# One hybrid decoder layer on one core: a reordered first stage, the sine product on another engine, a border with slices beside every maximum, and earlier fetches of the output weights

## The chip, the cores and the metric

The kernel runs on one core of a Trainium2 chip. The metric is the device time of one execution in microseconds. The kernel before was timed three times: 1210.0, 1212.68 and 1214.48 us, median **1212.68 us**. The profiled execution took 1212.92 us, of which 1211.0 us are the span from the first to the last instruction; 1.9 us lie around it.

Engines: PE is the matrix engine (PEld its weight loads), DVE is VectorE, ACT is ScalarE, POOL is GpSimd, SP is SyncE, which issues most of the DMAs.

## The reference, cut to what matters

A layer over 2048 tokens of width 1024 with two attention branches. Branch A (FoX) is causal attention of 8 heads with a forget-gate bias; branch B (SWA) is attention in a window of 128 tokens, with rotary positions and sinks. Each branch has a SiLU gate, and one output projection joins them.

```python
mod = silu(c) @ w_ada + b_ada                      # shift, scale, gate
h = rms_norm(x, g_pre) * (1 + scale) + shift
qa, ka, va, fa, za, qb, kb, vb, zb = split(h @ w_in)
oa = forgetting_attention(qa, ka, va, fa + b_fgate) * silu(za)
qb, kb = rope(qb, positions), rope(kb, positions)
ob = sliding_window_sink_attention(qb, kb, vb, sinks) * silu(zb)
y = concat(oa, ob) @ w_out
x = x + gate * rms_norm(y, g_post)
```

## The kernel before, in words

**Number form.** Every large product is done in three half-precision matmuls: an operand is split into a high and a low f16 part. A projection weight therefore passes through events: `w_load` (DMA on POOL's queue), `w_max` (largest magnitude, L213), `w_back`, `w_scale` (a power of two, L232 to L239), `w_high` (ACT, L247), `w_low` (DVE, L253), `w_done`.

**First stage** (written out by hand in program order, 0 to 59.2 us). Sixteen halves of `w_ada` (tiles `wa`, 512 KB each, L437) come in on SP's queue, with the positions `posi` (L443) and the rotary frequencies `ifr` (L444) issued behind the first of them, tokens x0 to x3 in the middle, then the first piece of the gate weight `wr_zb` (L207; POOL's queue fetches the same piece once before, at 4.36 us), then x4 to x7, which lie in memory named `hT` until they are used. PE and DVE sum the products of `w_ada` (L473, L482, closing sums L590 and L591). `squares(0)` (ACT, L374) and `root(0)` (13 small DVE instructions, L93 to L107) give the norm of x0 to x3, `normal(0)` scales the tokens (L384), and the small sums L592 to L629 end in the column scale `Gp` (L626) and shift `Shp` (L627). Then eight turns, one for each 128 of the 1024 columns: PE transposes (`px`, L392), ACT scales into `hT` and `hf` (L398), DVE makes the split (L402, L403); with them runs the projection `kb` of the first 512 tokens (L309).

**Projections** (59.2 to 127.1 us; token chunks ci = 0, 1, 2 of 512 tokens, the fourth up to 159 us). The work is a list of slices `punits`; a chunk is 8 slices `kb` (rotary keys), 8 slices `vb` (values and forget logits, L750), 8 slices of the gate `zb` (L309), and between them 8 `turn_x` slices that prepare the next chunk. `events` hangs other work on slice numbers: the weight events, and `squares`, `root` and `normal` of the next chunk. Evacuations are pushed ahead in `after(n, ...)`, and a tick releases the next of them; here there is a tick at every second slice. After the projection, `kb` and later `qb` go through `evac_rope`: ACT copies (`qf`, L707), SP swaps the halves by DMA (`qs`, L709), DVE multiplies by the cosine (L712), POOL multiplies by the sine (L721), DVE adds (L722), ACT makes the high part (L723), DVE the low (L716). Each engine takes its instructions in program order.

**SWA** (158.9 to 445.4 us): 32 windows with the other gate, query and value slices between them, with the same `evac_rope`. The prefix sums of the forget logits (`sums`, L791 and L792) come just ahead of it, at 149 us.

**Border** (445.4 to 494.6 us). Key rows (`lk`, L1203, transposed in L1183), one small sum of `w_out` (L1123), the first slices of the FoX head 0 (`qk0`, 32 slices of three matmuls with 512 columns each, their results swapped into T by DMAs from `stq`), the last value slices, and 34 maxima. A maximum is one matmul (L1226) and one DVE reduction (L1229 or L1231); they start 14 slices before the end of `qk0`, and FoX's first step waits for all of them.

**FoX** (to 1004 us): 160 steps, each with scores (L1275 to L1278), the exponential on ACT (L1282, L1286), the low part on DVE (L1289) and the products with values (L1299 to L1302), and filler slices spread over them. From 951 us, in head 6 and 7, pieces of `w_out` come in (`wo`, L1359 on SP) and are split (L1368 on ACT, then DVE), one a step; a piece is fetched two steps ahead of its split, at the end of a step. **Output** (to 1211 us): the last product (L1428) and norm.

Of the kernel before, what the change touches and what calls it, by code (L numbers as in the profile page):

```python
# [41 lines left out]
def hybrid_layer(  # L42
# [47 lines left out]
    def rsqrt_mean(dst, ss, n):  # L90

        v = sm(n, "rs_v")
# [6 lines left out]
        for it in range(3):  # L99
            t = sm(n, "rs_t")  # L100
# [6 lines left out]
            V.scalar_tensor_tensor(y2[:], t[:], 1.5, y[:], op0=ALU.add, op1=ALU.mult)  # L107
            y = y2
# [271 lines left out]
    def normal(ci, us=range(4)):  # L380
        for u in us:
            t, r = ci * 4 + u, rstd[ci][1][:, u:u + 1]
            if ci == 0 or (ci == 1 and u % 2):
# [39 lines left out]
    with tc.manual_schedule():  # L423
# [15 lines left out]
        for k in range(1):  # L439
            load_ada(1, k)  # L440

        for g in range(4):
            SP.dma_start(posi[32 * g:32 * g + 32, :], positions[0, g * CH:(g + 1) * CH].partition_broadcast(32))  # L443
        SP.dma_start(ifr[:], inv_freq)  # L444
        for k in range(1, KT):
            load_ada(1, k)
        make_identity(nc, ident)
        for key in first:
# [112 lines left out]
        w_load("zb0", pieces("zb0"), SP)  # L561
        for t in range(4, 8):
            load_x(t)
        ada_sum(1, True)

        mx3 = st.tile([P, 2], F32, name="mx3")
        for n, key in enumerate(first[:2]):
            V.tensor_reduce(mx3[:, n:n + 1], wq[key][0][:], axis=AX.XY, op=ALU.max, apply_absolute_value=True)
        ada_pe(0, 0, True)
        ada_pe(0, 3)  # L570
        PE.transpose(bk[0][0:2, 0:P], mx3[:], ident[:])
        ada_pe(0, 5)
        ada_dve(0, 1, True)
        ada_dve(0, 2, False)
        squares(0)
        scl0 = col8("scl0")
        ada_col(1, scl0)
        root(0)
        normal(0)
# [5 lines left out]
        ada_dve(0, 4, False)  # L585
        ada_dve(0, 6, False)

        for n in range(2):
            nn = slice(n * CH, (n + 1) * CH)
            PE.matmul(pm[0][n][:], ones[:], acc[0][:, nn], start=False, stop=False)  # L590
            PE.matmul(pm[0][n][:], silb[:, KT - 1, :], wa[0, KT - 1][:, nn], start=False, stop=True)  # L591
# [3 lines left out]
        w_scale("kb")  # L595
        w_high("kb")
        w_scale("vb")
        w_low("kb", 0, 1)
# [5 lines left out]
        V.scalar_tensor_tensor(absg[:], gcol[:], -1.0, gcol[:], op0=ALU.mult, op1=ALU.max)  # L604
        turned = [turn(0, k) for k in range(5)]
        squares(1)
        w_high("vb")
# [22 lines left out]
        w_low("vb", 0, 1)  # L630
        for k in range(KT):
            turned[k][0]()
            turned[k][1]()
            if k == 2:
                V.tensor_reduce(mxs[:, 2:3], wq["zb0"][0][:], axis=AX.XY, op=ALU.max, apply_absolute_value=True)
            if k + 5 < KT:
                turned.append(turn(0, k + 5))
        root(1)
        normal(1)
        spread(0)  # L640
        for key in ("kb", "vb"):
            kaps[key] = kappa(pws[key], key)
        V.tensor_scalar(kf[:], kaps["vb"][:], PS_SCALE, None, op0=ALU.mult)
    start.close()
# [52 lines left out]
    def evac_rope(ci, finish, pool):  # L697
        cols_ = slice(ci * CH, (ci + 1) * CH)

        def evac(ps, free):  # L700
# [20 lines left out]
            after(5, lambda: G.tensor_tensor(qs[:], qs[:], sinT[:, cols_], op=ALU.mult))  # L721
            after(6, lambda: V.tensor_tensor(qc[:], qc[:], qs[:], op=ALU.add))  # L722
            after(7, lambda: A.activation(stg[:, 0, :], qc[:], AF.Copy))  # L723
            after(8, low)
# [49 lines left out]
    def gates():  # L774
# [13 lines left out]
        def sums():  # L788
            lsf = nf[:].rearrange("p t h -> p (t h)")
            pc = bk[bank()][:]  # L790
            PE.matmul(pc[:, 0:P], triu[:], lsf, start=True, stop=True)  # L791
# [21 lines left out]
        after(4, sums)  # L813
# [132 lines left out]
    at_slice(6, z_row)  # L946
    at_slice(10, z_all)

    for ci in range(NCH):
# [3 lines left out]
        if ci < 3:  # L953
# [3 lines left out]
            at_ = [10, 12, 14, 16, 17, 18, 19, 20] if ci else [12, 14, 16, 17, 18, 19, 20, 21]  # L957
# [10 lines left out]
            if ci < 2:  # L968
                at_slice(n0 + 12, lambda ci=ci: [load_x(t) for t in range(4 * ci + 8, 4 * ci + 12)])
# [7 lines left out]
    N_PRO = len(punits)  # L977
    qbs = [(f"qb{c_ // 4}", qb_units(c_ // 4, c_ % 4)) for c_ in range(2, 16)]
# [84 lines left out]
    with swa_order:  # L1063
# [58 lines left out]
        pw_ = bk[bank()][:, 0:1]  # L1122
        PE.matmul(pw_, ones[:], wsum[:], start=True, stop=True)  # L1123
# [496 lines left out]
```

## Time and profile before

| part | us | what is to be seen |
|---|---|---|
| span of the profiled execution | 1211.0 | 1212.92 in all; median of three runs 1212.68 |
| PE busy | 1153.7 | 95% of the span |
| DVE busy | 908.2 | 75% |
| ACT busy | 662.0 | 55% |
| POOL busy | 142.1 | 12% |
| first stage | 0 to 59.2 | |
| projections, chunks 0 to 2 | 59.2 to 127.1 | |
| gates, first queries | 127.1 to 158.9 | |
| SWA | 158.9 to 445.4 | |
| border | 445.4 to 494.6 | |
| FoX | 494.6 to 1004.4 | |
| output | 1004.4 to 1211.0 | |

A row of the profile's timeline gives the start in us, the length in us, the engine, the line, the instruction with its output and inputs, its shape and the count, and in brackets how long the engine had been idle ahead of it and what ended that. Rows of an engine with "q" (SPq) are its issues of DMAs. A matmul's listed length is that of its pipeline, so it can overlap the next. The busy figures take that out.

### The profile page before, as it was taken

The numbers are of one execution on the slowest core, as the hardware profiler recorded it, in microseconds if no ns is written. First come the engines' busy times: TensorE is split into PE (matmuls) and PEld (weight loads), VectorE is DVE, ScalarE is ACT, GpSimd is POOL, SyncE is SP. The second block draws the span as 40 slices with busy tenths as digits, with TensorE's granted clock in tenths as the row PEclk, the third lists the DMA queues.
The fourth block names the chain that finished last, engine by engine and source line by source line (L and its number), as shares of the span: only waits on it lengthen the run. The fifth ranks groups of instructions, "written<-read, shape, count | busy, mean of one in ns | idle before, by whom it ended". The sixth has DMA issues, their size and how long they took to land.

```text
span 1211.0 us, 27262 instructions
## 1 busy us (share of the span) xinstructions
PE 1153.7 (95%) x10829; PEld 696.0 (57%) x10829; DVE 908.2 (75%) x2271; ACT 662.0 (55%) x1102; POOL 142.1 (12%) x252
## 2 busy tenths in 40 slices
PE   6789999999999989999999999999999899999997
PEld 2457545865558975555555555555555555555553
DVE  6866557676776645788899888987888887666665
ACT  2766436555555430466676666666676779433331
POOL 2011132223323210001100100001000000000000
PEclk9898999999999999999999999999999999999999
DMA  9554332323324323223422233212311336445652
GB/s 322 192 145 143 79 85 83 90 57 97 80 76 99 53 54 57 62 64 80 71 69 64 70 78 78 63 41 69 54 34 44 83 114 192 144 162 187 200 169 84
DMA packets 87723, 120.74 MB, mean 100 GB/s; under 512 B 27524, under 2 KB 63404, under 8 KB 87596
## 3 DMA queue, kind: packets, MB, share of 16 engines
q1 hardware_dynamic: 76520, 85.96, 24.3%
q0 software_dynamic: 10976, 33.03, 11.8%
q8 instruction: 85, 1.39, 0.6%
q14 instruction: 42, 0.34, 0.2%
q10 hardware_dynamic: 100, 0.02, 0.0%
HBM read 71.56 MB, written 25.18 MB: 80 GB/s over the span
## 4 chain that ended last, share of the span: by engine, by line
PE 53%; DVE 4%; ACT 1%; DMA 1%; issue 1%; SPq 0%; DVEq 0%; ACTq 0%
PE bk L309 17%; PE bk L1428 14%; PE sta L1276 4%; PE sta L1275 4%; PE bk L1226 4%; PE poa L1301 2%; PE poa L1302 2%; PE poa L1299 2%; DVE a_m L1229 1%; PE bk L1391 1%; DMA wo<-in_w_out_dram 1%; DVE pha L1289 1%; DMA T<-stq 1%; PE sta L1278 1%; ACT p L1282 0%
## 5 line engine op out<-in xcount | busy, mean ns | idle before, releaser
L1282 ACT ACTIVATE p<-sta,lift,scl_qk 128x1024 f32<-128x1024 f32 (+2 forms) x160 | 172.0, 1075 | 137.4 <-PE sta L1276 71.7
L309 PE MATMUL bk<-hT,wh_qk 128*128 128x512 f16 x768 | 198.2, 381 | 0.0
L1428 PE MATMUL bk<-wohl,oz 128*128 128x512 f16 x768 | 172.2, 379 | 0.7 <-DVE oz L1415 0.7
L1229 DVE TENSOR_REDUCE a_m<-bk 128x1 f32<-128x512 f32 x192 | 130.4, 687 | 56.4 <-PE bk L1226 52.0
L1289 DVE TENSOR_TENSOR pha<-p,pha 128x1024 f16<-128x1024 f32 (+2 forms) x160 | 168.9, 1056 | 0.2 <-ACT pha L1286 0.2
L1286 ACT ACTIVATE pha<-p 128x1024 f16<-128x1024 f32 (+2 forms) x160 | 147.8, 924 | 8.8 <-PE sta L1276 3.0
L1428 PEld LDWEIGHTS <-oz 128*128 128x128 f16 x768 | 74.3, 99 | 82.2 <-DVE oz L1415 1.2
L1299 PE MATMUL poa<-vt,pha 128*128 128x65 f16 x1088 | 116.4, 193 | 1.9 <-DVE ona L1308 1.9
L1302 PE MATMUL poa<-vt,pha 128*128 128x65 f16 x1088 | 116.0, 192 | 1.3 <-DVE pha L1289 1.0
L1301 PE MATMUL poa<-vt,pha 128*128 128x64 f16 x1088 | 116.4, 194 | 0.0
L309 PEld LDWEIGHTS <-wh_qk 128*128 128x128 f16 x768 | 72.5, 98 | 75.3 <-issue 2.9
L1275 PE MATMUL sta<-T 128*128 128x512 f16 (+1 forms) x320 | 110.9, 346 | 4.9 <-ACT p L1282 4.9
L1226 PE MATMUL bk<-T 66*128 66x512 f16 (+2 forms) x320 | 110.6, 349 | 4.4 <-DMA T<-stq 2.2
L1299 PEld LDWEIGHTS <-pha 128*128 128x128 f16 x1088 | 101.5, 96 | 16.3 <-DVE ona L1308 2.2
L1276 PE MATMUL sta<-T 69*128 69x512 f16 (+1 forms) x320 | 109.8, 348 | 0.0
L1301 PEld LDWEIGHTS <-pha 128*128 128x128 f16 x1088 | 100.9, 97 | 11.7
L1302 PEld LDWEIGHTS <-pha 128*128 128x128 f16 x1088 | 100.8, 99 | 1.3 <-DVE pha L1289 1.3
L309 PE MATMUL bk<-hT,wh_za 128*128 128x512 f16 x384 | 99.3, 378 | 0.0
L327 PE MATMUL bk<-wh_va,hT 128*128 128x128 f16 x1536 | 92.0, 220 | 0.6 <-issue 0.6
L327 PEld LDWEIGHTS <-hT 128*128 128x128 f16 x1536 | 88.7, 99 | 5.7 <-issue 3.4
L309 PE MATMUL bk<-hT,wh_zb 128*128 128x512 f16 x384 | 89.9, 379 | 1.1 <-DVE wh_zb L253 1.1
L309 PE MATMUL bk<-hT,wh_qb 128*128 128x512 f16 x384 | 87.2, 379 | 0.0
(495 smaller groups left out, 1877.3 us busy)
## 6 DMA issues: line engine op xcount, KB each, us to landing
hT<-in_x_dram SPq DMA_DIRECT2D x20, 512.0 KB
wa<-in_w_ada_dram SPq DMA_DIRECT2D x16, 512.0 KB
z_d<-tz POOLq DMA_DIRECT2D x32, 256.0 KB, 4.3
T<-stq SPq DMA_DIRECT2D x64, 128.0 KB
T<-o_d SPq DMA_DIRECT2D x16, 512.0 KB
T<-z_d SPq DMA_DIRECT2D x16, 512.0 KB
out_dram<-hT SPq DMA_DIRECT2D x15, 512.0 KB
xt<-in_x_dram SPq DMA_DIRECT2D x12, 512.0 KB
```

What stands on the lines that cost most here:

```text
L309: PE.matmul(ps, whl[:, a, k, :], hT[ci][:, b, k, :], start=(k == 0 and n == 0), stop=(k == KT - 1 and n == 2))
L327: PE.matmul(ps[:, u * P:(u + 1) * P], hT[ci][:, a, k, u * P:(u + 1) * P], whl[:, b, k, :], start=(k == 0 and n == 0), stop=(k == KT - 1 an ...
L1226: PE.matmul(mx[:, :w], T[0:XM, 0, i * P:(i + 1) * P], T[0:XM, 2, pc * CH:pc * CH + w], start=True, stop=True)
L1275: PE.matmul(self.st[:, o:o + w], T[:, 3, kb_], T[:, 1, qc], start=True, stop=False)
L1276: PE.matmul(self.st[:, o:o + w], T[0:XR, 2, kb_], T[0:XR, 0, qc], start=False, stop=not diag)
L1282: A.activation(self.p32[:, :self.w], self.st[:, :self.w], AF.Exp, scale=scl[f"qk{self.hd}"][:], bias=lift[:])
L1286: A.activation(self.ph[:, 0, :self.w], self.p32[:, :self.w], AF.Copy)
L1289: V.tensor_tensor(self.ph[:, 1, :self.w], self.p32[:, :self.w], self.ph[:, 0, :self.w], op=ALU.subtract)
L1299: PE.matmul(po[:, u, :], ph[:, 0, pq], vt[:, b, hd, 0:65], start=(self.first and n == 0 and u == 0), stop=False)
L1301: PE.matmul(po[:, u, 0:64], ph[:, 0, pq], vt[:, b, hd, 65:VW], start=False, stop=False)
L1302: PE.matmul(po[:, u, :], ph[:, 1, pq], vt[:, b, hd, 0:65], start=False, stop=(self.last and n == len(self.blocks) - 1))
L1428: PE.matmul(py, self.hl[:, i, k, :], w_slot(8 * j + k)[:, cc], start=(k == 0 and m_ == 0), stop=(k == KT - 1 and m_ == 2))
```

## The change

1. **First stage.** `posi` and `ifr` go to ACT's queue. POOL's first load of `wr_zb` is gone, and the one on SP stands behind x4 to x7. The maximum over the weights and both `w_scale` come ahead of `root(0)`; both `w_low` come after the last `w_ada` product, ahead of the turns. `squares(1)` stays behind; `root(1)` is spread over the turns (`rsqrt_parts` yields three times); the maximum of `wr_zb` moves behind the turns; `normal(1)` is all on VectorE, two of its four inside slices 13 and 14. x8 to x11 are loaded at the stage's end, x12 to x15 at slice 1.
2. **Rotary positions.** The sine product moves from GpSimd (after 5 ticks) to VectorE (after 7), in front of the addition; the high and low parts come one tick later.
3. **Projections.** `squares`, `root`, `normal` of chunk ci + 2 move into chunk ci, turn slots spread out, weight events of the split one or two slices earlier.
4. **Gates' sums** become a generator, called in four portions at slices N_PRO + 20, 23, 26 and 29.
5. **Border.** Four slices come ahead of the key rows, the small sum of `w_out` behind them; maxima begin 12 slices before the end of `qk0` and every one has a slice beside it; a tick comes at every slice. The border so takes six slices that FoX's steps had.
6. **Pieces of `w_out`** are fetched three steps ahead, in the middle of a step.

```diff
-    after(5, lambda: G.tensor_tensor(qs[:], qs[:], sinT[:, cols_], op=ALU.mult))
-    after(6, lambda: V.tensor_tensor(qc[:], qc[:], qs[:], op=ALU.add))
-    after(7, lambda: A.activation(stg[:, 0, :], qc[:], AF.Copy))
-    after(8, low)
+    def sine():
+        V.tensor_tensor(qs[:], qs[:], sinT[:, cols_], op=ALU.mult)
+        V.tensor_tensor(qc[:], qc[:], qs[:], op=ALU.add)
+    after(7, sine)
+    after(8, lambda: A.activation(stg[:, 0, :], qc[:], AF.Copy))
+    after(9, low)
...
-        after(4, sums)
+        fx["sums"] = sums()
...
-            at_ = [10, 12, 14, 16, 17, 18, 19, 20] if ci else [12, 14, 16, 17, 18, 19, 20, 21]
+            at_ = [6, 8, 10, 12, 14, 16, 18, 20] if ci else [14, 16, 17, 18, 19, 20, 21, 22]
-            if ci:
+            if ci < 2:
                 for u in range(4):
-                    at_slice(n0 - 9 + 2 * u, lambda ci=ci, u=u: squares(ci + 1, (u,)))
-                    at_slice(n0 + 3 + u, lambda ci=ci, u=u: normal(ci + 1, (u,)))
-                at_slice(n0 + 2, lambda ci=ci: root(ci + 1))
+                    at_slice(n0 + (3 if ci else 9) + u, lambda ci=ci, u=u: squares(ci + 2, (u,)))
+                    at_slice(len(punits) - (5 if ci else 10) + u, lambda ci=ci, u=u: normal(ci + 2, (u,)))
+                at_slice(len(punits) - 13, lambda ci=ci: root(ci + 2))
...
+    for n in range(4):
+        at_slice(N_PRO + 20 + 3 * n, lambda: next(fx["sums"], None))
...
+        fill(4, tick)
         key_rows(0)
-        fill(8, tick2)
+        pw_ = bk[bank()][:, 0:1]
+        PE.matmul(pw_, ones[:], wsum[:], start=True, stop=True)
+        root_scale(wrt[:], pw_)
         while pos[0] < N_V3 or mi < M_LEAD:
-            if pos[0] < N_V3:
-                fill(1)
-            if mi < M_LEAD and pos[0] >= N_QK0 - 14:
+            fill(1)
+            if mi < M_LEAD and pos[0] >= N_QK0 - 12:
                 munits[mi]()
                 mi += 1
-            tick2()
+            tick()
...
             tick()
+            for m in w_at.get(s + 3, []):
+                w_out_load(m)
...
-                here = list(range(s + 2, 7 * NS))[:KT]
+                here = list(range(s + 3, 7 * NS))[:KT]
...
-            for m in w_at.get(s + 2, []):
-                w_out_load(m)
+                w_out_load(0)
```

The end of the first stage's loads on SP, in the program's order (`wa` are halves of `w_ada`, `hT_110` is the memory that holds x4 to x7, `cosT` the first use of the queue after the loads). Before:

```order
L437 DMA wa_286<-in_w_ada_dram 128x1024
L437 DMA wa_288<-in_w_ada_dram 128x1024
L207 DMA wr_zb_290<-in_w_in_dram 128x8x128
L367 DMA hT_110<-in_x_dram 128x1024 x4
L417 DMA cosT<-cs__244 32x512
```

Of the change:

```order
L442 DMA wa_284<-in_w_ada_dram 128x1024
L442 DMA wa_286<-in_w_ada_dram 128x1024
L372 DMA hT_110<-in_x_dram 128x1024 x4
L212 DMA wr_zb_292<-in_w_in_dram 128x8x128
L422 DMA cosT<-cs__242 32x512
```

The tokens now stand ahead of `wr_zb`. The four `posi` and the `ifr`, which stood behind the first `wa` of this queue, are no longer on it.

ACT in the projections. Here `xt_667` to `xt_673` before and `xt_530` to `xt_536` after are the tokens x8 to x11; `hT_108` is the second chunk's turned input. Before, a piece inside the turns of the second chunk:

```order
L398 ACTIVATE hT_108<-px,Shp,Gp 128x512
L398 ACTIVATE hf<-px,Shp,Gp 128x512 x2
L374 ACTIVATE junk,ss<-xt_667 128x1024
L398 ACTIVATE hT_108<-px,Shp,Gp 128x512
L398 ACTIVATE hf<-px,Shp,Gp 128x512
L374 ACTIVATE junk,ss<-xt_669 128x1024
L398 ACTIVATE hf<-px,Shp,Gp 128x512
L374 ACTIVATE junk,ss<-xt_671 128x1024
```

Of the change, from the first chunk's key copy `qf` on:

```order
L710 ACTIVATE qf<-bk_137 128x512
L379 ACTIVATE junk,ss<-xt_530 128x1024
L379 ACTIVATE junk,ss<-xt_532 128x1024
L379 ACTIVATE junk,ss<-xt_534 128x1024
L764 ACTIVATE vb<-bk_138 128x2x64 x2
L379 ACTIVATE junk,ss<-xt_536 128x1024
L252 ACTIVATE wh_zb_702<-wr_zb_292,w_sw 128x1024
L403 ACTIVATE hT_108<-px,Shp,Gp 128x512
```

The squares of the chunk after next now stand ahead of the turns, no longer between them.

PE at the start of the border, weight loads included; `lk` are the key rows, `w_mx` the sum of `w_out`, `wh_qk` the weight of the FoX head's queries and keys. Before:

```order
L893 MATMUL pob<-vb,ptb 128x64
L1123 MATMUL bk_139<-w_mx_6601,ones 128x1
L1183 LDWEIGHTS lk
L1183 MATMUL bk_137<-identh,lk 72x128
L309 LDWEIGHTS wh_qk_6459
L309 MATMUL bk_138<-hT_107,wh_qk_6459 128x512
```

Of the change, from the twelfth matmul of `qk0` behind the last `pob` on:

```order
L314 LDWEIGHTS wh_qk_6457
L314 MATMUL bk_137<-hT_107,wh_qk_6457 128x512
L1197 LDWEIGHTS lk
L1197 MATMUL bk_138<-identh,lk 72x128
L1514 MATMUL bk_139<-w_mx_6599,ones 128x1
L314 LDWEIGHTS wh_qk_6457
L314 MATMUL bk_137<-hT_107,wh_qk_6457 128x512
```

Twelve matmuls of `qk0` (four slices) now lie between the last product of SWA and the key rows, and the sum of `w_out` comes behind these.

More of the change, by code (lines that the diff above doesn't have):

```diff
@@ L90, in rsqrt_mean, with rsqrt_parts @@
     def rsqrt_mean(dst, ss, n):
+        for _ in rsqrt_parts(dst, ss, n):
+            pass
+    def rsqrt_parts(dst, ss, n):
         v = sm(n, "rs_v")
@@ L382, in normal @@
             t, r = ci * 4 + u, rstd[ci][1][:, u:u + 1]
-            if ci == 0 or (ci == 1 and u % 2):
+            if ci == 0:
                 A.activation(xt[t], xt[t], AF.Copy, scale=r)
@@ L568, in hybrid_layer @@
             V.tensor_reduce(mx3[:, n:n + 1], wq[key][0][:], axis=AX.XY, op=ALU.max, apply_absolute_value=True)
+        PE.transpose(bk[0][0:2, 0:P], mx3[:], ident[:])
         ada_pe(0, 0, True)
-        ada_pe(0, 3)
-        PE.transpose(bk[0][0:2, 0:P], mx3[:], ident[:])
-        ada_pe(0, 5)
         ada_dve(0, 1, True)
         ada_dve(0, 2, False)
[L575 to L579, printed above, removed]
         m3 = st.tile([2, 1], F32, name="m3")
@@ L584, in hybrid_layer @@
         PE.matmul(bk[0][:, P:P + 2], ones[0:2, :], dg3[:], start=True, stop=True)
[L585 to L591, printed above, removed]
+        ada_pe(0, 3)
+        ada_pe(0, 5)
+        squares(0)
+        scl0 = col8("scl0")
+        ada_col(1, scl0)
         V.tensor_copy(mxs[:, 0:2], bk[0][:, P:P + 2])
@@ L595, in hybrid_layer @@
         w_scale("kb")
+        w_scale("vb")
         w_high("kb")
-        w_scale("vb")
-        w_low("kb", 0, 1)
+        w_high("vb")
         scl1 = col8("scl1")
@@ L604, in hybrid_layer @@
         V.scalar_tensor_tensor(absg[:], gcol[:], -1.0, gcol[:], op0=ALU.mult, op1=ALU.max)
+        root(0)
+        normal(0)
+        ada_dve(0, 4, False)
+        ada_dve(0, 6, False)
+        ada_pe(0, KT - 1)
+        ada_sum(0, True)
+        w_low("kb", 0, 1)
+        w_low("vb", 0, 1)
         turned = [turn(0, k) for k in range(5)]
         squares(1)
-        w_high("vb")
         shf0 = col8("shf0")
@@ L633, in hybrid_layer @@
             turned[k][1]()
-            if k == 2:
-                V.tensor_reduce(mxs[:, 2:3], wq["zb0"][0][:], axis=AX.XY, op=ALU.max, apply_absolute_value=True)
+            if k >= 2:
+                next(root1, None)
             if k + 5 < KT:
                 turned.append(turn(0, k + 5))
-        root(1)
-        normal(1)
-        spread(0)
+        V.tensor_reduce(mxs[:, 2:3], wq["zb0"][0][:], axis=AX.XY, op=ALU.max, apply_absolute_value=True)
         for key in ("kb", "vb"):
@@ L643, in hybrid_layer @@
         V.tensor_scalar(kf[:], kaps["vb"][:], PS_SCALE, None, op0=ALU.mult)
+        normal(1, (0, 1))
+        spread(0)
+        for t in range(8, 12):
+            load_x(t)
     start.close()
@@ L944, in z_all @@
         wq["zb0"].append(mxs[:, 2:3])
-    at_slice(6, z_row)
-    at_slice(10, z_all)
+    at_slice(10, z_row)
+    at_slice(12, z_all)
+    for u in (2, 3):
+        at_slice(11 + u, lambda u=u: normal(1, (u,)))
+    at_slice(1, lambda: [load_x(t) for t in range(12, 16)])
     for ci in range(NCH):
@@ L1121, in hybrid_layer @@
         V.tensor_reduce(wsum[:], wst[:], axis=AX.X, op=ALU.add)
-        pw_ = bk[bank()][:, 0:1]
-        PE.matmul(pw_, ones[:], wsum[:], start=True, stop=True)
-        root_scale(wrt[:], pw_)
     swa.close()
```

32 lines of the change are left out of this document (18 added, 14 removed).

## The prediction

> **What bounds the kernel now.** The windows view comes first: one row for each stage, with its length, then busy time and instruction count of PE, PEld, DVE, ACT and POOL, then the granted PE clock, the DMA share and GB/s.
>
> ```profile
> core 0: us, PE busy (x) PEld busy (x) DVE busy (x) ACT busy (x) POOL busy (x), PEclk, DMA share, GB/s
> 0.00:49.60 49.60, 30.81 (x75) 13.82 (x76) 33.09 (x82) 21.23 (x32) 7.14 (x17) 0.96 0.90 313
> 49.60:59.20 9.60, 8.90 (x40) 4.75 (x40) 9.25 (x20) 7.34 (x11) 0.00 (x0) 0.83 0.01 3
> 59.20:74.20 15.00, 14.80 (x155) 11.81 (x152) 11.57 (x38) 11.11 (x19) 1.27 (x1) 1.00 0.53 155
> 74.20:103.40 29.20, 23.36 (x177) 16.24 (x176) 17.80 (x42) 19.18 (x34) 1.93 (x2) 0.88 0.55 164
> 103.40:127.10 23.70, 22.00 (x177) 15.70 (x176) 17.93 (x44) 14.13 (x26) 4.11 (x6) 0.93 0.36 90
> 158.90:445.40 286.50, 284.64 (x3334) 198.67 (x3333) 198.05 (x564) 151.91 (x417) 80.53 (x153) 1.00 0.33 79
> 445.40:494.60 49.20, 41.96 (x327) 25.13 (x327) 30.10 (x93) 7.09 (x14) 5.06 (x8) 0.93 0.22 41
> 956.00:1004.40 48.40, 41.79 (x487) 25.66 (x485) 41.72 (x79) 38.80 (x48) 1.08 (x2) 1.00 0.41 123
> ```
>
> PE sets the time: in SWA it is idle for 1.9 us of 286.5. It is idle for 18.8 us in the first 49.6, for 0.2 + 5.8 + 1.7 = 7.7 us in the projections, for 7.2 us in the border and 6.6 us in the stretch of the `w_out` pieces. No multiplication goes away, so the change can only win such time, and the time that a halved clock takes beside it:
>
> ```profile
> 83.60:87.01 3.41, 1.19 (x17) 0.85 (x14) 3.10 (x14) 0.00 (x0) 0.49 (x1) 1.00 0.54 160
> 87.01:93.84 6.83, 5.43 (x38) 4.72 (x39) 4.66 (x8) 2.26 (x5) 1.34 (x1) 0.50 0.48 100
> 448.83:452.24 3.41, 3.41 (x10) 1.21 (x9) 0.00 (x0) 0.25 (x1) 0.00 (x0) 0.50 0.04 7
> 476.13:479.55 3.42, 3.42 (x27) 2.70 (x25) 1.24 (x2) 0.86 (x2) 0.07 (x1) 0.50 0.36 43
> ```
>
> After a window in which PE worked 1.19 of 3.41 us, the clock stood at 0.50. Half of the busy time in such a row is lost: 2.7 us at 87, 1.7 at 448.8 and 1.7 at 476.1; in the third chunk a clock of 0.93 over 23.7 us loses another 1.7. Projections: 7.7 idle + 2.7 + 1.7 = **12.1 us** lost. Border: 7.2 + 3.4 = **10.6 us**.
>
> **First stage.** Rows of the timeline:
>
> ```profile
> 2.64 2.53 SPq L443 DMA_DIRECT2D posi<-in_positions_dram  x4
> 13.00:36.00 23.00, 17.82 (x33) 7.38 (x34) 19.29 (x38) 7.93 (x15) 0.00 (x0) 0.93 1.02 408
> 32.46 0.17 DVE L93 TENSOR_SCALAR rs_v<-ss 128x4 f32<-128x4 f32 x1 [1.24 <-ACT junk L374]
> 32.51 3.61 PE L473 MATMUL bk<-wa,silb 128*128 128x512 f32 x4 [3.58 <-DMA wa<-in_w_ada_dram]
> 34.65 0.16 DVE L107 SCALAR_TENSOR_TENSOR rst<-rs_t,rs_y 128x4 f32<-128x4 f32 x1
> 36.27 0.28 DVE L581 TENSOR_REDUCE m<-bk 2x1 f32<-2x128 f32 x1 [1.46 <-PE bk L571]
> 39.36 1.13 PE L590 MATMUL bk<-acc,ones 128*128 128x512 f32 x2 [1.10 <-DVE acc L482]
> 46.67 1.06 ACT L374 ACTIVATE junk<-hT 128x1024 bf16<-128x1024 f32 x1 [1.55 <-DMA hT<-in_x_dram]
> 52.89 1.21 DVE L635 TENSOR_REDUCE mxs<-wr_zb 128x1 f32<-128x1024 f32 x1
> ```
>
> The DMA engines are full (share 1.02) and PE waits 3.58 us for a half of `w_ada`: loads come first. One 0.52 MB piece of `wr_zb` less at 408 GB/s is 1.3 us. The four `posi` held SP for 2.53 us ahead of the second `wa`; I count 1.0 of it, nearer to the lower end because the engines are full soon after. Loads: 2.3 us (0 to 3.8). The second `wr_zb` piece behind x4 to x7 gives those tokens, for which ACT waited at 46.67, another 1.3 us, so they will not end last. On DVE, the m reduction waited 1.46 us after `root(0)` (ended 34.81) and held the last two `acc`, for which PE waited 1.10. With m moved ahead, the `acc` follow the root directly: they began at 36.7 (36.27 + 0.28 and a 0.2 us product) and would at 34.8, 1.9 us sooner. The two `w_scale` that come ahead of the root fit in its 1.24 us wait for the squares and the shift of the position work. What is late next is `acc` itself. Against this stands `root(1)` between the splits: 13 instructions took 32.46 to 34.81, 2.35 us; the 1.21 us maximum of `wr_zb` leaves the loop; of the 1.1 that is left I count 0.7 as not hidden by ACT's scaling. `posi` and `ifr` on ACT's queue cost at most their 2.5 us of issue there, and ACT works for only 21.2 of the first 49.6 us. First stage: 2.3 + 1.9 - 0.7 = **3.5 us** (1 to 6).
>
> **Projections.** PE rows at three stalls, then two groups of the lines view from 59.2 to 127.1 (busy us, mean ns):
>
> ```profile
> 79.56 0.59 PE L309 MATMUL bk<-hT,wh_kb 128*128 128x512 f16 x2 [1.02 <-DVE hT L403]
> 86.39 0.30 PE L392 MATMUL px<-ident,xt 128*128 128x128 f32 x1 [1.95 <-DVE xt L386]
> 111.65 0.30 PE L392 MATMUL px<-ident,xt 128*128 128x128 f32 x1 [0.76 <-DVE xt L386]
> L403 DVE TENSOR_TENSOR hT<-hf,hT 128x512 f16<-128x512 f32 x24 | 16.6, 691 | 12.6 <-ACT hf L398 12.2
> L386 DVE TENSOR_SCALAR xt<-xt,rst 128x1024 f32<-128x1024 f32 x8 | 6.5, 875 | 0.1
> ```
>
> The transposes wait for `normal`, 1.95 us and more, and so does the clock. Done a chunk ahead, `normal` ends before the turns begin: the stalls and halvings at 86 and 111 go. The splits waited 12.2 us for ACT, whose squares (1.06 us each, as at 46.67) stood between the scalings; those go too. What is late next is DVE in the first chunk. Its 11.57 us of 15.0 gain two `normal` (1.75), root(2) (2.35) and two `normal` of x8 to x11 (1.75), the maximum of `wr_zb` (1.2), the last splits and the sine (0.7): about 20 against PE's 14.8, so some 5 us are late there, as the 1.02 wait at 79.56 was; half of it moves into the next chunk. Over all three chunks DVE has 11.57 + 17.80 + 17.93 = 47.3 us and 2.1 of sine against PE's 60.2 less 4.4, 55.8: it fits, with little to spare. I give the new stall 2.5 us in the first chunk and 2.7 us to fills between, so of 12.1 us come back **6.9 us** (0 to 9).
>
> The clock needs a choice: a leftover 2.5 us in one window of 3.41 us would leave PE 0.9 us busy, less than the row at 83.60, and so cost 1.7 more. I expect it spread over several splits and take none; the range holds it. [...]
>
> **Sine.** From the lines view of SWA:
>
> ```profile
> L721 POOL TENSOR_TENSOR qs<-qs,sinT 128x512 f32<-128x512 f32 x15 | 19.1, 1270 | 14.1 <-DMA qs<-qf 14.0
> L722 DVE TENSOR_TENSOR qc<-qc,qs 128x512 f32<-128x512 f32 x15 | 10.2, 683 | 9.0 <-POOL qs L721 8.9
> ```
>
> Fifteen products of 1.27 us on POOL become fifteen of 0.68, the price of the neighbouring addition of the same shape: 10.2 us more on DVE, which is idle for 88 us of SWA. Its 8.9 us of waiting for POOL go. PE's idle time there is 1.9 us, the most to win; I take 0.
>
> **Gates' sums** and the split that stood behind them:
>
> ```profile
> 149.20 0.46 PE L791 MATMUL bk<-nf,triu 128*128 128x128 f32 x2 [0.68 <-DVE nf L786]
> 156.61 2.33 PE L309 MATMUL bk<-hT,wh_zb 128*128 128x512 f16 x10 [1.11 <-DVE wh_zb L253]
> ```
>
> In portions well behind `nf`, and with the split's events a slice or two earlier, both waits go: **1.8 us** (0 to 1.8). The bank that the portions hold is one of several; PE takes others meanwhile.
>
> **Border.**
>
> ```profile
> 446.97 0.38 PE L1123 MATMUL bk<-w_mx,ones 128*128 128x1 f32 x2 [1.55 <-DVE w_mx L1121]
> 448.52 0.25 PE L1183 MATMUL bk<-identh,lk 128*72 128x128 f16 x1 [1.17 <-DVE lk L1203]
> 471.68 0.81 PE L309 MATMUL bk<-hT,wh_qk 128*128 128x512 f16 x3
> 472.54 0.81 PE L309 MATMUL bk<-hT,wh_qk 128*128 128x512 f16 x3
> 475.56 0.39 PE L1226 MATMUL bk<-T 66*128 66x512 f16 x1 [2.21 <-DMA T<-stq]
> 494.38 0.38 PE L1226 MATMUL bk<-T 66*128 66x512 f16 x1 [1.23 <-DVE a_m L1229]
> ```
>
> Opening: 1.55 + 1.17 and the halving at 448.8, 4.4 us. Twelve matmuls between (ten of the shape took 2.33 us at 156.61, so 2.8 us) cover DVE's chain to 448.5; I keep 0.5 for what they do not, 3.9 won. Middle: 2.21 and its halving 1.7. Maxima begin two slices later, and a tick at each slice evacuates `stq` sooner: from one slice to the next with a maximum between it is 0.86 us (471.68 to 472.54), so T has some 3 us more. I count 3.5. End: six slices now stand beside the last maxima, which had none; DVE (30.1 us of 49.2) has also splits there, so I count 0.5 of 1.23. Sum **7.9 us** (4 to 10.6). The six slices are missing from FoX's filler: the same work elsewhere, and no gain.
>
> **Pieces of `w_out`.**
>
> ```profile
> 965.06 0.38 PE L1275 MATMUL sta<-T 128*128 128x512 f16 x1 [2.04 <-ACT p L1282]
> 985.99 0.72 ACT L1368 ACTIVATE wohl<-wo,wsc 128x512 f16<-128x512 f32 x1 [2.50 <-DMA wo<-in_w_out_dram]
> 988.69 0.27 PE L1275 MATMUL sta<-T 128*128 128x256 f16 x1 [1.41 <-ACT p L1282]
> ```
>
> ACT stood 2.50 us at a split, and PE behind it 1.41; the wait of 2.04 has the same cause one split earlier. FoX's 160 steps take 509.8 us (494.6 to 1004.4), 3.2 each, so a fetch one step and a half ahead of the old one covers both. But SP issues in order, and an output's DMA can still stand ahead; I count **2.5 us** of 3.45 (0 to 4).
>
> **Sum.** 3.5 + 6.9 + 0 + 1.8 + 7.9 + 2.5 = 22.6 us. 1212.9 less 22.6 is 1190.3; the profiled run lies 0.2 above the median, so **1190 us**.
>
> **Rivals.** (a) DVE becomes the bound of the projections. For it: about 20 us of work against 14.8 in the first chunk; against it: the sum over three chunks. C gives nothing: 1197. (b) The border's last wait only changes its name: DVE's reductions, splits and scales, or T's DMA, hold PE as before. For it: the row at 475.56 is a DMA; against it: DVE is idle 19 us there. Border 3.9 for 7.9: 1194. (c) Loads do not move: PE waits for the same halves, the first stage gives 1, and `w_out` 0 because the queue is behind, not the fetch: 1212.9 - 17.6 = 1195. (d) **Slower.** DVE takes instructions in order, and the sine now waits there for the swap by DMA. Behind it stand the window's maxima, for them the exponentials on ACT and then PE. From 1.5 us a product (22.6 / 15) the gain is gone, from 1.9 the kernel is slower by over 0.5%; at 2.2 it is 1212.9 - 22.6 + 33 = 1223. For it: POOL waited 14.0 us in 15 swaps, 0.9 each; against it: two more ticks pass first, and POOL had little else to do. (e) The stages shift but each wait returns in the next, the change does not do what it says: 1207 to 1213.
>
> **How the numbers follow.** Forecast 0.42, (a) 0.17, (b) 0.14, (c) 0.12, two of these three together 0.08 (about 1200), (d) 0.03, (e) 0.04. The best ends of all terms give 6 + 9 + 1.8 + 10.6 + 4 = 31, 1181; two rivals and some of the third reach 1203. Range 1181 to 1203. A measurement of this kernel can tell about 0.5%, 6 us, from no change: faster 0.92, same 0.05, slower 0.03.
>
> **What would show it.** In the changed profile: the last square of the first stage near 43 instead of 46.67, and `kb` of the first chunk ended at 55 to 56; no stall on `normal` ahead of a transpose and a clock of 1.00 from 75 to 120, the end of the third `zb` near 117; no wait at the sums; no halved clock at the border's start and middle; no wait of ACT for `wo`; DVE without waits for `qs` in SWA. A DVE that is busy without a gap in the projections while PE waits for splits would make (a) right; waits of DVE for `qs` by DMA beside PE idle in SWA, (d).

## The result and the profile after

The changed kernel took **1203.54 us** (median of four runs, 1201.86 to 1204.70) beside 1212.24 for the kernel before in four runs: ratio 0.9927, 95% interval 0.9905 to 0.9950. That is 8.7 us won where 22.6 were forecast, half a microsecond outside the range. The span of its profiled execution is 1202.7 us, 8.3 below that of before, so the stages must account for 8.3.

The windows view of the changed kernel, cut at the same places of the program as that of before (columns as there):

```profile
0.00:56.20 56.20, 39.36 (x112) 18.24 (x113) 42.37 (x108) 28.68 (x42) 6.12 (x16) 0.91 0.84 293
56.20:114.90 58.70, 55.94 (x509) 40.04 (x508) 46.57 (x118) 41.94 (x73) 2.70 (x4) 1.00 0.44 124
114.90:148.20 33.30, 29.37 (x209) 16.26 (x207) 16.60 (x52) 10.78 (x19) 4.93 (x9) 1.00 0.37 84
148.20:435.60 287.40, 285.28 (x3338) 199.20 (x3339) 208.81 (x593) 152.12 (x418) 60.80 (x138) 1.00 0.34 79
435.60:479.10 43.50, 41.42 (x340) 24.71 (x339) 32.21 (x98) 7.14 (x14) 4.72 (x7) 1.00 0.26 57
```

FoX is best cut at its exponentials, which have the same numbers in both kernels: the first stands at 495.7 before and 480.2 after, that of step 132 at 949.4 and 941.8, the last at 1037.4 and 1028.5 (the output's first products already run beside the last ones).

| stage | before, us | after, us | won | forecast |
|---|---|---|---|---|
| first stage | 59.2 | 56.2 | 3.0 | 3.5 |
| projections, three chunks | 67.9 | 58.7 | 9.2 | 6.9 |
| gates, first queries | 31.8 | 33.3 | -1.5 | 1.8 |
| SWA | 286.5 | 287.4 | -0.9 | 0 |
| border | 49.2 | 43.5 | 5.7 | 7.9, less the work moved in |
| FoX, exponential of step 0 to 132 | 453.7 | 461.6 | **-7.9** | the work moved out |
| step 132 to the last exponential | 88.05 | 86.67 | 1.4 | 2.5 |
| the rest | 173.6 | 174.2 | -0.6 | 0 |

The 1.1 us between the border's end and the first exponential are in no row; they are the same in both.

At FoX's start the change was 15.5 us ahead, with 15 matmuls of FoX already done. It gave 7.9 of that back in a stretch that the forecast had written off in one sentence.

**Where FoX lost it.** PE's waits there, before and after (engine, tile and line, what was waited for: us in total, times, longest us):

```profile
PE poa L1299 <- DVE ona L1308: 1.9, 2, 1.0
PE bk L1226 <- DVE a_ri L1306: 0.4, 1, 0.4
```

```profile
PE bk L1240 <- DMA T<-rw: 7.4, 3, 3.0
PE bk L1240 <- DVE ona L1322: 1.5, 1, 1.5
```

The wait for `T<-rw`, the DMA of a head's key rows, is new. A maximum of the next head needs them. Here is the worst of these waits in the timeline of the changed kernel, rows of POOL's and SP's queues and of PE:

```profile
837.90 0.57 POOL L221 DMA_DIRECT2D mx_d<-w_mx  x1 [21.21 <-DVE w_mx L218]
839.23 1.30 SPq L1203 DMA_DIRECT2D T<-rw  x2
847.84 0.27 PE L1240 MATMUL bk<-T 66*128 66x128 f16 x1 [2.95 <-DMA T<-rw]
```

and the same place before:

```profile
852.21 1.30 SPq L1189 DMA_DIRECT2D T<-rw  x2
853.21 0.57 POOL L216 DMA_DIRECT2D mx_d<-w_mx  x1 [22.12 <-DVE w_mx L213]
857.63 0.22 PE L1226 MATMUL bk<-T 66*128 66x128 f16 x1
```

`mx_d` is the first half of `w_max`: the largest magnitude of each partition, 128 words, goes out to be read back as one row. Before, the key rows were issued first; now `mx_d` is. The pair of issues is two DMAs: the first brings two rows, which the maximum reads, the second a third row, which it doesn't. PE comes to this matmul about as soon after the pair's issue in both (4.1 us behind its end before, 4.4 after), so PE isn't early; the rows are late. From the semaphore events of the trace, end of issue to landing: the first DMA 1.3 us before (852.89 to 854.14) and 7.8 after (839.91 to 847.71, with PE starting at 847.84), the second 1.1 before (853.51 to 854.63) and 7.4 after (840.53 to 847.95). `mx_d` itself landed at 846.45. (In three of the seven heads before, `mx_d` went out beside the pair, at 648.83 for instance with the pair at 648.51 and 649.24. There the second of the pair landed with it, at 656.75, but the first, the one that PE needs, at 650.45, and PE, which came at 653.25, did not wait.) The DMA view of the changed kernel from 825 to 850 us (count, KB, median us to landing):

```profile
mx_d<-w_mx POOLq DMA_DIRECT2D x2, 0.5 KB, 7.9
```

Half a kilobyte is under way for 7.9 us, and small DMAs issued behind it, on another queue, land late too. In the runs of this case the second DMA of a pair, whose landing has events of all 16 DMA engines, was issued 47 times while an `mx_d` was under way, and each time it landed 0.2 to 6.2 us after that `mx_d`. The first DMA uses fewer engines (its landing at 847.71 has three events) and was once let off (issued at 772.50 in the changed kernel, landed at 775.04, with `mx_d` at 777.41). (At two of the four waits, 503.06 and 640.77, a fetch of 512 KB named `gw` was also under way, issued just behind `mx_d`; at the other two it was not.)

The trace's records of DMA packets show where the time goes. The 16 packets of `mx_d` had all started by 839.2, those of the pair and of the DMA just ahead of it on SP's queue, `o_d`, by 841.4. In the stretch that follows none of these DMAs has landed in full, and the DMA engines record no work:

```profile
841.50:845.00 3.50, 3.40 (x26) 1.57 (x24) 3.47 (x6) 1.81 (x3) 0.56 (x1) 1.00 0.00 0
```

So the rows do not wait for their turn to start. What is late is the landing.

The packets of the rows had started (by 841.4) while `mx_d` had not landed (846.45), and the rows landed after it (847.71 and 847.95). Why `mx_d` itself lands so late no run shows, nor why the rows land behind it.

Such a wait can also halve the clock. Windows of 3.41 us, cut where the clock changes, around that wait, and the one that holds most of the equally long wait before 640.77:

```profile
843.78:847.19 3.41, 1.11 (x6) 0.29 (x3) 3.24 (x10) 1.90 (x3) 1.02 (x2) 1.00 0.28 66
847.19:850.61 3.42, 2.77 (x33) 2.40 (x34) 1.20 (x4) 0.91 (x2) 0.08 (x1) 0.50 0.48 63
850.61:854.02 3.41, 3.41 (x11) 1.38 (x10) 1.44 (x3) 0.55 (x2) 0.54 (x1) 0.50 1.35 30
638.98:642.39 3.41, 1.62 (x26) 1.26 (x27) 1.70 (x4) 0.26 (x1) 0.00 (x0) 1.00 1.01 259
```

PE worked 1.11 of 3.41 us and then ran at half speed for 6.8 us, which loses half of 2.77 + 3.41, 3.1 us: the wait cost 6, not 3. The other wait left 1.62 us of work in its window, and the clock stayed at 1.00 behind it.

The account of FoX: PE's gaps of over 0.05 us grew from 2.5 to 10.0 us, 7.5 more, of which the waits for rows are 1.47 + 2.95 + 1.46 + 2.95 = 8.8 (that of 1.46, put down to `ona`, ended 0.13 us after its rows landed); the halved clock took 3.1. Against that stand 15 matmuls less, 3.2 us at 0.65 us for three. 7.5 + 3.1 - 3.2 = 7.4, of the 7.9.

**Gates.** The timeline of the changed kernel: the weight events of `qb0` on POOL and DVE, then PE at the first query slices and at the first scores of SWA:

```profile
101.88 0.91 POOL L212 DMA_DIRECT2D wr_qb<-in_w_in_dram  x1
109.92 0.69 POOL L221 DMA_DIRECT2D mx_d<-w_mx  x1 [7.13 <-DVE w_mx L218]
118.18 0.54 POOL L226 DMA_DIRECT2D mxr<-mx_d  x1 [7.56 <-DMA mx_d<-w_mx]
...
123.56 0.28 DVE L237 TENSOR_REDUCE w_mx<-mxr 128x1 f32<-128x128 f32 x1 [5.88 <-DMA mxr<-mx_d]
...
128.40 5.34 PE L314 MATMUL bk<-hT,wh_qb 128*128 128x512 f16 x24 [2.51 <-DVE qc L715]
...
148.11 0.29 PE L852 MATMUL pss<-kst,stb 64*128 64x128 f16 x4 [1.42 <-ACT stb L729]
```

From the load at 101.88 to the first matmul at 128.40 are 26.5 us, most of them three DMAs one after the other. Its events are placed by slice number, and the projections in front of it now take 9.2 us less: PE is there before the weight.

### The profile page after: what moved, and what is told of

The parts are those of the page before. It is cut to its first block, busy times and chain, and to the rows that moved or that the text cites. A ratio compares the mean times of both kernels' runs of the same rounds, so it can differ in the third digit from the quotient of the medians.

```text
span 1202.7 us, 27228 instructions
## 1 busy us (share of the span) xinstructions
PE 1150.1 (96%) x10829; PEld 692.2 (58%) x10829; DVE 918.0 (76%) x2293; ACT 662.3 (55%) x1100; POOL 114.8 (10%) x231
## 4 chain that ended last, share of the span: by engine, by line
PE 77%; DVE 8%; DMA 7%; issue 6%; ACT 2%; POOL 0%; SPq 0%; DVEq 0%; ACTq 0%; POOLq 0%
PE bk L314 28%; PE bk L1442 13%; PE bk L332 7%; PE sta L1290 4%; PE sta L1289 4%; PE bk L1240 4%; PE poa L1315 3%; PE poa L1313 3%; PE poa L1316 3%; DMA T<-rw 2%; PE pxb L885 2%; DMA wa<-in_w_ada_dram 2%; PE pss L852 2%; PE pob L904 2%; DVE a_m L1243 1%
## 5 line engine op out<-in xcount | busy, mean ns | idle before, releaser
L314 PE MATMUL bk<-hT,wh_qk 128*128 128x512 f16 x768 | 195.0, 378 | 0.0
L1240 PE MATMUL bk<-T 66*128 66x512 f16 (+2 forms) x320 | 110.4, 349 | 10.5 <-DMA T<-rw 7.4
```

Of the source, the lines that this page charges most:

```text
L314: PE.matmul(ps, whl[:, a, k, :], hT[ci][:, b, k, :], start=(k == 0 and n == 0), stop=(k == KT - 1 and n == 2))
L1240: PE.matmul(mx[:, :w], T[0:XM, 0, i * P:(i + 1) * P], T[0:XM, 2, pc * CH:pc * CH + w], start=True, stop=True)
```

## The experiments

Each kernel was timed beside the kernel before (median 1210.6 to 1211.7 there). "FoX" is the time from the first exponential to that of step 132: 453.7 us before, 461.6 after. Six kernels have the new border and its maxima where the change puts them on GpSimd's queue; their profiles give 458.9 to 465.1 us, so some 3 us between two of them can be scatter. The four kernels below that move the maxima back or keep the border of before give 452.8 to 453.3.

### Are the late key rows the loss in FoX?

**Maxima later**, in the changed kernel: the `w_max` and `w_back` of the FoX weights, all but the first, six and five slices later, so that the rows go first.

```diff
                     lead -= 1
+                if n in (1, 2) and key[:2] in ("qk", "za") and key != "qk0":
+                    lead -= 6 if n == 1 else 5
```

> The changed kernel with one thing different: for the weights of FoX (heads 1 to 7 and their gates) the maximum with its DMA out comes 6 slices later and its DMA back 5 slices later, so that the DMA of 128 words of 4 bytes stands behind the DMA of the key rows again, as it did before. Theory 1 (the six slices that the border took shift the slice-numbered weight events ahead of the step-numbered key rows, and that slow DMA holds the key rows up): the four waits of PE for T<-rw or T in FoX (1.47, 2.95, 1.46 and 2.95 us, 8.8 in all) go, 1203.5 - 8.8, about 1195 us. Theory 2 (PE reaches the first maximum of a head sooner because fewer filler slices stand beside it, the row DMA is as slow as ever): the waits stay, 1203.5 us within 2.

1199.84 us (ratio 0.9904, 0.9887 to 0.9921). No wait for rows is left, and FoX takes 453.3. But the border became 2.8 us longer, with a new wait on DVE and, behind it, on PE:

```profile
466.37 0.29 DVE L237 TENSOR_REDUCE w_mx<-mxr 128x1 f32<-128x128 f32 x1 [3.66 <-DMA mxr<-mx_d]
...
468.27 1.44 PE L332 MATMUL bk<-wh_va,hT 128*128 128x128 f16 x12 [2.50 <-DVE a_m L1245]
```

DVE takes instructions in order: it stood 3.66 us at the row that comes back from `w_max` of a border weight, with reductions that PE needed behind it. So the order of these events is the cause in FoX, and the first few weights should not have been moved.

**The border as before**, in the changed kernel, with all else kept (`w_out`'s small sum too):

```diff
-        fill(4, tick)
         key_rows(0)
...
+        fill(8, tick2)
         while pos[0] < N_V3 or mi < M_LEAD:
-            fill(1)
-            if mi < M_LEAD and pos[0] >= N_QK0 - 12:
+            if pos[0] < N_V3:
+                fill(1)
+            if mi < M_LEAD and pos[0] >= N_QK0 - 14:
```

> The changed kernel with the border of before (no slice beside the last maxima, a tick at every second slice, the small sum of w_out ahead). Theory 1: the border loses its 9.5 us again, FoX gets its 8.8 us of waits back, so the time hardly moves: 1202 to 1206 us, with no wait for T<-rw in FoX. Theory 2 (FoX's waits come from another part of the change): the border's 9.5 us are lost and FoX's waits stay, about 1213 us.

1199.01 us (0.9897, 0.9878 to 0.9916), less than either theory had. FoX starts 4.0 us later than in the changed kernel (484.2) and takes 452.8, without a wait for rows. The new border wins in its own stage and loses more in FoX: as shipped it costs 4.5 us.

**Kernel before, maxima six slices earlier**, to make the same waits there:

```diff
+                if n in (1, 2) and key[:2] in ("qk", "za") and key != "qk0":
+                    lead += 6
```

> The kernel before with one thing different: for the weights of FoX (heads 1 to 7 and their gates) the maximum with its DMA out and the DMA back come 6 slices earlier. Theory 1: the DMA of 4-byte words now stands ahead of the key rows as in the changed kernel, waits of PE for T<-rw appear, and the time grows by 6 to 10 us to 1218 to 1222. Theory 2 (the order of these DMAs does not matter): 1212 us within 2.

1212.72 us (1.0012, 0.9998 to 1.0025): theory 1 missed. In six heads an `mx_d` now stood 4.5 to 10.5 us ahead of the rows. The DMA that PE needs landed 1.7 to 5.2 us after its issue in five of them and 7.9 in one, where before it was 1.3. PE's waits for rows were 1.88 and 0.82 us, and a halved clock took 1.7. The profile, which is of the slowest of the twelve runs, has FoX at 458.2. So six slices early are not free, but they cost far less than one slice early, which comes next.

**Kernel before, maxima one slice earlier**, so that `mx_d` goes just ahead:

```diff
+                if n in (1, 2) and key[:2] in ("qk", "za") and key != "qk0":
+                    lead += 1
```

> The kernel before with the FoX maxima and their way back one slice (about 1.4 us) earlier, so that the 4-byte DMA stands just ahead of the key rows, where e3 had it 6 to 10 us ahead. Theory 1 (the rows land with that DMA, about 8 us after its issue, and PE reaches them 4 to 5 us after theirs): waits for T<-rw of 1 to 3 us in about five heads, 1217 to 1222 us. Theory 2 (the order of these DMAs does not matter, as e3's time suggests): 1212 us within 2.

1223.04 us (1.0093, 1.0074 to 1.0111). Up to FoX this kernel runs as before (its first exponential 1.6 us earlier), then FoX takes 467.6 us. PE's waits there:

```profile
PE bk L1228 <- DMA T<-rw: 6.8, 3, 3.1
PE bk L1228 <- DVE a_m L1231: 4.0, 6, 1.2
PE bk L1228 <- DVE a_m L1240: 2.0, 1, 2.0
```

The three waits for rows and the one of 2.0 (it ended 0.14 us after its rows landed) make 8.8 us, as much as in the changed kernel, and nothing of the change is in this one but the earlier events. No fetch of `gw` was under way at any of the four. They are not all of it: the moved events also put small waits for DVE there, 4.0 us, and two halved clocks cost 3.1.

**`mx_d` on SP's queue**, in the changed kernel: is it the queue of GpSimd that is slow?

```diff
-        G.dma_start(md[:], mx[:])
+        SP.dma_start(md[:], mx[:])
```

> The changed kernel with the DMA of the 128 maxima of a weight (mx_d, 4 bytes each) issued by SP in place of GpSimd. Theory 1 (the queue of GpSimd makes that DMA take 8 us and hold others): it lands in about 2.5 us, the waits for T<-rw in FoX and the late query weight at 125.9 go, about 1193 us. Theory 2 (128 words of 4 bytes written to memory take 8 us on any queue and hold the rows behind them): the waits for T<-rw stay or grow, 1203 us or more. SP waits in order for each maximum, which can cost up to 2 us by itself.

1204.39 us (0.9944, 0.9926 to 0.9962), as the changed kernel (FoX 4.3 us shorter, but begun 6.1 us later; what it lost ahead of FoX was not followed). `mx_d` still took 6.6 to 9.8 us to land, and the rows were still late:

```profile
840.61 0.34 SPq L221 DMA_DIRECT2D mx_d<-w_mx  x1
...
842.21 1.31 SPq L1203 DMA_DIRECT2D T<-rw  x2
```

PE waited 2.99 us for these, at 850.87. So it isn't only GpSimd's queue. Nor is it DRAM as the target alone: `o_d` (128 KB in pieces of 256 bytes, also to DRAM) landed 1.6 us after its issue where no `mx_d` was out (852.11 to 853.74 in the kernel before). Whether it is the pieces of four bytes was not tried.

### The gates, and both repairs together

**`qb0` ten slices earlier** (load, maximum and way back), in the changed kernel:

```diff
+                if n < 3 and key == "qb0":
+                    lead += 10
```

> The changed kernel with the load, maximum and maximum's way back of the first query weight (qb0) 10 slices earlier. Theory 1 (the chain load, maximum, DMA out, DMA back, scale, split takes about 26 us whatever the slices do, and PE now arrives 12 us sooner): the wait of 2.51 us of PE at 125.9 goes, 1203.5 - 2.5, about 1201 us. Theory 2 (PE waits there for VectorE's in-order work, the cosine product that frees the bank): the wait stays within 0.5 us and the time within 1 us.

1199.92 us (0.9901, 0.9883 to 0.9919). The waits of 2.51 and 1.42 are gone, SWA's first exponential is 14.3 us ahead of before (9.9 in the changed kernel). FoX still waits 8.3 us for rows: 5.7 in three waits, and one of 2.6 that is put down to DVE but ended 0.14 us after its rows landed.

**Both**: `qb0` early, and maxima later for all but `qk0`, `qk1` and `za0`, whose place the border's wait had shown to be right.

```diff
+                if n in (1, 2) and key[:2] in ("qk", "za") and key not in ("qk0", "qk1", "za0"):
+                    lead -= 6 if n == 1 else 5
+                if n < 3 and key == "qb0":
+                    lead += 10
```

> The changed kernel with the later maxima of e1_max_later for the FoX weights from head 2 on (head 1 and the first gate keep their places, since in e1 a scale waited for the late DMA there, 2.50 us of PE) and the earlier qb0 chain of e4_qb0_early. If the two causes are independent their gains add: 1203.5 - 4.5 - 6 to 8, about 1192 us. If one hides the other: no better than e4, 1199 us. Head 1's rows at 495 still stand behind a DMA of 4-byte words, so a wait of 1 to 1.5 us stays there.

**1191.54 us** (0.9831, 0.9816 to 0.9846), 20 us below the kernel before and the fastest of all. FoX takes 452.9, and no wait for rows is left. It has 15 matmuls less than before, 3.2 us, and is only 0.8 us shorter: 1.8 of the difference are other gaps, 4.2 us in place of 2.5.

**`qb0` early, border as before**, which prices the new border when nothing is late behind it:

> The kernel of e4_qb0_early with the border of before, to read what the new border is worth beside e7_both_chains (1191.5), which has the new border and no late key rows. Theory 1 (the border itself wins 7.9 us, of which 3.9 are work taken over from FoX, so some 4 to 8 us in the end): 1195 to 1199 us, and no wait for T<-rw. Theory 2 (the new border is worth nothing even without the late rows): 1191.5 us within 1.5.

1194.84 us (0.9870, 0.9850 to 0.9890): 3.3 us slower than both repairs together. That is what the border is worth; its own stage shows 5.7.

### The other terms

**Sine back on GpSimd**, in the changed kernel:

```diff
-            after(7, sine)
-            after(8, lambda: A.activation(stg[:, 0, :], qc[:], AF.Copy))
-            after(9, low)
+            after(5, lambda: G.tensor_tensor(qs[:], qs[:], sinT[:, cols_], op=ALU.mult))
+            after(6, lambda: V.tensor_tensor(qc[:], qc[:], qs[:], op=ALU.add))
+            after(7, lambda: A.activation(stg[:, 0, :], qc[:], AF.Copy))
+            after(8, low)
```

> The changed kernel with the sine product back on GpSimd, at the old ticks. Theory 1 (the sine on VectorE cost nothing and won nothing; the waits at 125.9 and 148 come from the late query weight): 1203.5 us within 1.5, the wait of 2.51 at 125.9 stays. Theory 2 (the sine on VectorE, in order and one tick later, is behind the waits at 125.9 and 148): these shrink by 2 us or more, about 1201 us.

1211.85 us (1.0004, 0.9991 to 1.0017): the whole gain gone, which neither theory had. The lines view from 55 to 160 us, of this kernel and of the changed one (busy us, mean ns, then the idle time ahead and its cause):

```profile
L725 DVE TENSOR_TENSOR qc<-qc,qs 128x512 f32<-128x512 f32 x5 | 3.5, 692 | 15.1 <-POOL qs L724 15.1
```

```profile
L725 DVE TENSOR_TENSOR qs<-qs,sinT 128x512 f32<-128x512 f32 x6 | 4.1, 686 | 4.7 <-DMA qs<-qf 4.6
```

DVE stood 15.1 us at the addition. Of these, 4.2 are in the projections (2.6 at 67, 1.6 at 114) and 10.8 at the first queries behind them, where the kernel before already waits 7.4. The splits stand behind the addition, and behind the first of these waits PE stood too:

```profile
75.11 0.59 PE L314 MATMUL bk<-hT,wh_kb 128*128 128x512 f16 x2 [1.12 <-DVE hT L408]
76.78 0.38 PE L314 MATMUL bk<-hT,wh_kb 128*128 128x512 f16 x1 [1.07 <-DVE hT L407]
```

The clock was halved again behind these (77.1 to 80.6 us). PE comes to the first query slices 2.4 us later than in the changed kernel, SWA's first exponential is 4.1 later and FoX's 5.2. FoX itself takes 3.5 more, with 11.4 us of waits for rows in place of 8.8, which can be scatter in part.

**Sine on GpSimd, addition a tick later** (`G.tensor_tensor` at `after(5)`, `V.tensor_tensor` at `after(7)`, the rest as in the changed kernel):

> The changed kernel with the sine product on GpSimd at tick 5 as before, but VectorE's addition at tick 7 and the rest as in the change. In e5_sine_gpsimd the addition at tick 6 made VectorE wait 15.1 us for GpSimd between 55 and 160 us, and the kernel took 1211.85. Theory 1 (the tick of the addition is what matters: VectorE, in order, was asked for it too early): most of the 8.3 us are back, 1203 to 1206 us. Theory 2 (the engine matters: GpSimd's product waits for the tables and for its own queue of DMAs, so VectorE waits at tick 7 too): 1208 to 1212 us.

1207.44 us (0.9968, 0.9954 to 0.9981), about half way back. DVE still waits for POOL, less:

```profile
L725 DVE TENSOR_TENSOR qc<-qc,qs 128x512 f32<-128x512 f32 x6 | 4.1, 687 | 7.5 <-POOL qs L724 7.5
```

So of the 8.3 us about half (4.4) is the later tick and half (3.9) the engine.

**`w_out` two steps ahead**, at the end of a step, as before:

```diff
-            for m in w_at.get(s + 3, []):
-                w_out_load(m)
...
-                here = list(range(s + 3, 7 * NS))[:KT]
+                here = list(range(s + 2, 7 * NS))[:KT]
...
+            for m in w_at.get(s + 2, []):
+                w_out_load(m)
```

> The changed kernel with the pieces of w_out fetched two steps ahead, at the end of a step, as before. Theory 1 (the earlier fetch won what the prediction says): PE's idle time in the stretch of the pieces grows by 2 to 3 us, about 1206 us, with ACT waiting for wo again. Theory 2 (VectorE's splits are what PE waits for there, the fetch is hidden): 1203.5 us within 1.

1202.50 us (0.9933, 0.9911 to 0.9956): the earlier fetch is worth nothing that can be measured. ACT's wait for a piece returns:

```profile
952.27 0.72 ACT L1382 ACTIVATE wohl<-wo,wsc 128x512 f16<-128x512 f32 x1 [1.83 <-DMA wo<-in_w_out_dram]
```

but PE has hardly more idle time with it: 4.6 us from step 132 to the last exponential, against 4.3 in the changed kernel. The kernel before has 6.6 there, but the two kernels of before with earlier maxima, whose fetch is the old one too, have 4.1 and 3.9. In this kernel PE waits 2.39 us for ACT's `p`; in the changed one it waits 2.28 us for DVE, a few us on:

```profile
960.17 0.32 PE L1197 MATMUL bk<-identh,lq 128*72 128x128 f16 x1 [2.28 <-DVE lq L1260]
```

DVE has no gap of over 0.4 us from 947 to 963 us there.

**First loads as before**, in the changed kernel (`posi` and `ifr` on SP, `wr_zb` twice and ahead of x4 to x7):

```diff
-        A.dma_start(ifr[:], inv_freq)
...
-            A.dma_start(posi[32 * g:32 * g + 32, :], positions[0, g * CH:(g + 1) * CH].partition_broadcast(32))
+            SP.dma_start(posi[32 * g:32 * g + 32, :], positions[0, g * CH:(g + 1) * CH].partition_broadcast(32))
...
-        for key in first[:2]:
+        for key in first:
...
+        w_load("zb0", pieces("zb0"), SP)
         for t in range(4, 8):
             load_x(t)
-        w_load("zb0", pieces("zb0"), SP)
```

> The changed kernel with the loads of the first stage as before: positions and frequencies on SP behind the first half of w_ada, the first piece of the gate weight fetched twice, and ahead of x4 to x7. Theory 1 (the loads carry 2.3 us of the first stage, as the prediction has it): the first key projection ends 2 to 3 us later, at 58 to 59, 1206 us. Theory 2 (the order on VectorE carries the gain): it ends within 1 us of 56.2, 1203.5 to 1204.5 us.

1205.97 us (0.9965, 0.9951 to 0.9979), with the first stage 2.5 us longer: the loads are worth 2.4 us.

## Why the prediction was wrong, step by step

- **First stage**, 3.5 forecast, 3.0 measured: right, and its loads, 2.3 of it, were confirmed on their own (2.4), against rival (c). The reordered m reduction and the spread root were not tried apart.
- **Projections**, 6.9 forecast, 9.2 measured: right in mechanism, and the new stall was sized too high. PE's idle time fell from 7.7 to 2.8 us, and the clock stands at 1.00 in the whole row from 56.20, where two halvings had cost 4.4. Rival (a), a DVE that binds, did not come: no wait for a split is over 0.55 us. The choice to charge no halved clock held.
- **Sine, "I take 0"**: wrong. It was priced by PE's idle time in SWA alone. In the projections, where the change leaves DVE and PE little to spare, an addition that waits for POOL holds the splits behind it on DVE. With the product back on GpSimd the kernel takes 8.3 us more: 2.4 are lost before the first query slices, so part of what the row above won hangs on the sine; then 1.7 at the first queries, 1.1 on the way to FoX and 3.5 in FoX. Rival (d), DVE held by the swap, did not come. In SWA of the changed kernel DVE's waits ahead of the fifteen products are 0.1 us in all:

```profile
L725 DVE TENSOR_TENSOR qs<-qs,sinT 128x512 f32<-128x512 f32 x15 | 10.2, 681 | 0.1
```

- **Gates**, 1.8 forecast, -1.5 measured: its two waits, 0.68 and 1.11 us, did go, but two of 2.51 and 1.42 came. The step failed that let the time shrink in front of a chain of DMAs and left the chain its slice number. Rival (e) had it in words, "each wait returns in the next", and named no place.
- **SWA**, 0 forecast, -0.9 measured. PE is busy 0.6 us longer in the new row, with four matmuls more; the rest was not looked into.
- **Border**: its waits and halved clocks were 7.2 + 3.4 = 10.6 us and are 43.50 - 41.42 = 2.1 now, with a clock of 1.00, so 8.5 won for 7.9 forecast. Right; rival (b) did not come.
- **"The six slices are missing from FoX's filler: the same work elsewhere, and no gain."** This is the sentence that failed, and the main error. The work is the same, but the weight events too are placed by its slice numbers, while the key rows go by FoX's steps. With six slices done in the border, the `w_max` events in FoX moved ahead of rows that they had stood behind or beside, and hold them. That took waits of 8.8 us and 3.1 of halved clock; with the maxima moved back, FoX is 8.3 us shorter (461.6 to 453.3), and in the kernel before one slice of shift makes the same waits.
- **`w_out`**, 2.5 forecast, 1.4 measured in that stretch, none of it shown to come from the fetch: kernels with the old fetch have as little idle time there. The wait for the piece was on ACT, but DVE's dense work stood next to it and took its place. (Its 3.2 us a step was also low, since FoX's last step lies at 1037.4: it is 3.4.)

Of the 14.3 us that are missing, border and FoX together make 10.1, the gates 3.3, `w_out` 1.1 and smaller terms 2.0; the projections gave 2.3 more than forecast. Even so, the sum was nearly there to be had: with the two tables of lead numbers put right the same change gives 20 us of the 22.6. What was missed are two chains of DMAs whose numbers the change did not carry along.

## What to carry to other kernels

When work is moved between two places, look for what is counted by that work: events hung on a slice number move against those hung on a step number, and two that were in a safe order can swap. When a stall goes ahead of a chain of DMAs that takes as long as before (from the issue of `qb0`'s `mx_d` to the read of `mxr` 13.6 us in both kernels), that chain's lead in slices becomes shorter in time and must be lengthened, and a tiny DMA just ahead of one that the matrix engine waits for can hold it: here the rows landed 7.8 us after their issue behind half a kilobyte, in place of 1.3. Price an instruction that moves between engines by what stands behind it in order at its tightest place, and not by the idle time of the stage where there are most of them.

## What the runs showed of the hardware that was not expected

A DMA of 128 words of four bytes from SBUF to DRAM took 6.2 to 9.5 us from the end of its issue to its landing on POOL's queue, and 6.6 to 9.8 on SP's. A small DMA on all 16 engines that was issued while it was under way landed after it in all 47 cases, most of them on another queue; the pair shown took 7.4 us in place of 1.1. There the packets of both had started by 841.4, 6 us before the pair landed, so it is the landing that is late. Why the 128 words land so late stays open.

In the changed kernel the clock halved after a window of 3.41 us in which PE had worked 1.11 us (843.78 to 847.19), and did not after one with 1.62 us (638.98 to 642.39). No sharp limit follows from that: in the kernel before it halved at 114.32, after a window with 1.73 us of work.
